# One block of gate and up by Strassen's scheme, SiLU as one ScalarE pass, and exchanges issued by GpSimd

## The chip, the core and the metric

The kernel runs on one core of a Trainium2 chip. The engines meant below are TensorE (PE, matmuls; its weight loads are listed as PEld), VectorE (DVE), ScalarE (ACT), GpSimd (POOL) and SyncE (SP, which here only issues DMAs). The metric is the device time of one execution in microseconds; three runs of the kernel before gave 575.81 us in the median (575.01 to 576.74).

## The reference, cut to what matters

One decoder layer on 256 tokens of width 1024, all in float32. The parts that the change touches are the feed-forward network (width 2816) and the gate at the end:

```python
x = x + (sigmoid(g_a) * y_a + sigmoid(g_b) * y_b) @ W_out
h2 = rms_norm(x, ln2_g[i])
g_ff, u_ff = jnp.split(h2 @ w_gate_up[i], 2, axis=-1)
x = x + (jax.nn.silu(g_ff) * u_ff) @ w_down[i]
h3 = rms_norm(x, ln3_g[i])
x = x + (p[i] @ w_ple_proj[i]) * jax.nn.sigmoid(h3 @ w_ple_gate[i])
```

`w_gate_up` is 1024 x 5632: 2816 columns of gate, then 2816 of up.

## The kernel before

**Matmuls in three terms.** Every float32 operand is split into a rounded high part (`wh`, `ah`) and the remainder (`wl`, `al`), and a product is the sum of three matmuls, `ah wh + ah wl + al wh` (`Panel.step`, issued by `mm` at L275). The tokens stand in two halves of 128, the columns in panels of 512, the inner dimension in pieces of 128. A panel holds one PSUM bank for each token half. Two pieces of weights, 128 x 2 x 512, make a tile: SP loads it (L395), ACT rounds it into `wh` (all ACT passes are recorded at L254), DVE subtracts to get `wl` (L377). Four buffers hold raw tiles, five `wh`, five `wl`. A tile serves 12 matmuls of 512 columns in an ordinary panel: two pieces, two token halves, three terms.

**Order.** The program text is written around PE. A filler (`Filler`) keeps a modelled time that each matmul advances, and runs side tasks (generators that yield the time at which they want to go on) between matmuls. The engines' queues are then laid out by priority: "w" (weight tiles) ahead of "ev" (work on finished panels) ahead of "bg" (background) ahead of the matmuls, each instruction as early as a model of the time finds it ready. Each engine executes its queue in order, so an instruction that waits holds all behind it.

**Gate and up** (L1497 to L1583). The feed-forward columns are cut into five blocks of 512 and one of 256. The first three panels (gate and up of block 0, gate of block 1) run interleaved; from then on `whole()` runs one panel as two halves of four pieces each. For the gate, `Gated.gate` takes a sigmoid on ACT with the row's `rstd2` as scale, and a DVE instruction multiplies the scaled panel with it (L1509). For up, one DVE instruction multiplies the panel in (L1518), DVE transposes within 32 x 32 blocks (L1527), and `send` moves the 32-row groups among the partitions with 16 DMAs from SP (L1537), so that the columns come to stand on partitions. After a lag of 26 us of modelled time `split` rounds the moved block (ACT) and takes the remainder (DVE, L1549), and the down projection can use it. Only after the last block's rows are split can the last chunk of the first down panel run.

**Norms.** `h2` is not divided by its row norm before the matmuls; the factor `rstd2` (one number per token, so two columns of 128) is applied to the finished panels. `rstd3` is used in the same way at the end.

**The end.** `pj` holds `p @ w_ple_proj`, copied from PSUM at L1489 long before. `final` (L1598) takes the sigmoid of the last panels on ACT, multiplies with `pj` (L1603), adds the residual (L1604) and stores.

Of the kernel before, what the change touches and what calls it, by code (L numbers as in the profile page):

```python
# [16 lines left out]
P = 128  # L17
# [46 lines left out]
NFF = 11  # L64

# [124 lines left out]
def tile_layer(ctx: ExitStack, tc: tile.TileContext, head, xk, pt, vec, w_dt, w_big, w_dn2, w_pp, out):  # L190
# [171 lines left out]
    def w_tiles():  # L362
        return (sb.tile([P, 2, 512], F32, tag="raw", bufs=RAW, name=nm("raw")),
                sb.tile([P, 2, 512], F32R, tag="wh", bufs=WH, name=nm("wh")),
                sb.tile([P, 2, 512], F32R, tag="wl", bufs=WL, name=nm("wl")))
# [1053 lines left out]
    class Residual:  # L1419
# [7 lines left out]
        def take(self, n, pan):  # L1427
# [51 lines left out]
    for n in range(2):  # L1479
        pan = Panel()  # L1480
        parts = load(w_pp[n], 2)
        for tt, pc in enumerate(pan.pieces):
            for k in range(2):
                pan.step(pc, parts[k], (p_h[:, k], p_l[:, k]), k == 1)
                if 4 * n + 2 * tt + k in SPLITS:
                    res2.split(*ready.pop(0))
        with prio("ev"):
            for tt in range(2):
                copy = nc.vector.tensor_copy(pj[n][:, tt], pan.ps[tt])  # L1489
                if n == 1:  # L1490

                    follow(copy.ins, fill.split)


    ff = []

    class Gated:  # L1497
# [4 lines left out]
        def gate(self, pan, c):  # L1502

            with prio("ev"):
                for tt, ps in enumerate(pan.ps):
                    r = rstd2[:, tt : tt + 1]
                    f = s2([self.w])
                    act(f, ps[:, c], AF.Sigmoid, scale=r)
                    stt(f, ps[:, c], r, f, op0=ALU.mult, op1=ALU.mult)  # L1509
                    self.f.append(f)  # L1510
# [20 lines left out]
        def send(self, turned):  # L1531
            n = self.both.shape[3]
            moved = s4([4, 2 * n])
            with prio("ev"):
                for a in range(4):
                    for b in range(4):
                        nc.sync.dma_start(  # L1537
                            moved[32 * b : 32 * b + 32, a], self.both[32 * a : 32 * a + 32, b].rearrange("p t n -> p (t n)"))
            fill.spawn(self.split(moved.rearrange("p a (x j) -> p x a j", j=32)), 0)

        def split(self, moved):

            yield fill.now + (26000.0 if self.w > 256 else 26500.0)
# [7 lines left out]

    behind = iter([(None, None), (fill.rounded, fill.rounded)])
    pans = [Panel(), Panel(aside=True), Panel()]
# [9 lines left out]

    def whole():
# [6 lines left out]
    gated = Gated(512)  # L1571
    gated.gate(pans[0], WHOLE)
    gated.up(pans[1], WHOLE)
    for n in range(1, NFF // 2):
# [3 lines left out]
    pan = Panel()  # L1578
    for k in (0, 4):
        pan.add(next_chunk(), h2[k : k + 4], last=k == 4)  # L1580
# [4 lines left out]
    res3 = Residual(xin, V_G3, rstd3, False)  # L1585
    for n in range(2):
# [11 lines left out]
    def final(n, pan):  # L1598
        with prio("ev"):
            for tt, c, ps in pan.pieces:  # L1600
                t = s2([512])[:, c]
                act(t, ps, AF.Sigmoid, scale=rstd3[:, tt : tt + 1])
                nc.vector.tensor_mul(t, t, pj[n][:, tt, c])  # L1603
# [6 lines left out]
def _layout(i):  # L1610
# [36 lines left out]
    blocks[:2] = [[np.concatenate(pairs[k : k + 2], axis=1) for k in range(0, 12, 2)], blocks[1][2:]]  # L1647
    rest = np.concatenate([w[:, 512 * (NFF // 2) :][:, :256] for w in (gu, ups)], axis=1)
# [41 lines left out]
```

## Time and profile before

| | |
|---|---|
| median of three runs | 575.81 us (575.01 to 576.74) |
| the profiled execution | 574.76 us, span 572.8 us |
| granted TensorE clock | 1.0 |
| PE busy | 567.3 us, 99% of the span |
| weight loads busy | 476.0 us, 83% |
| DVE busy | 444.5 us, 78% |
| ACT busy | 339.7 us, 59% |
| POOL busy | 88.0 us, 15% |
| DMA | 121.22 MB, mean 212 GB/s |

The trace gives each instruction with its line, its start from the span's beginning, its duration, and the idle time of its engine before it with what ended that idle time. A row such as `1.06 ACT ... [1.66 <-PE g L275]` says that ACT ran 1.06 us after 1.66 us without work, and that PE at line 275 released it. Matmul durations overlap, because they are pipelined; the distance between their starts is what one costs.

### The profile page before, as it was taken

The page shows a single profiled execution, that of the slowest core. Times are in us where ns is not written, and L with a number is a line of the kernel's source. Part 1 is how long each engine was busy: PE and PEld are TensorE (multiplying, and loading weights), DVE is VectorE, ACT ScalarE, POOL GpSimd, SP SyncE. Part 2 cuts the span into 40 slices and gives each one's busy share as a digit, 9 for nine tenths or more (in the row PEclk, how much of TensorE's full clock was granted, in tenths as well). Part 3 has the DMA queues.
Part 4 walks back from the last instruction along what each step waited for, and adds up shares of the span by engine and source line. Part 5 has one row for each costly group of instructions (what it writes and reads, how often), then busy time and mean ns, then how long its engine had stood idle before and what let it go on. Part 6 is the DMA issues. An engine that isn't in the chain of part 4 may idle for free.

```text
span 572.8 us, 8553 instructions
## 1 busy us (share of the span) xinstructions
PE 567.3 (99%) x2971; PEld 476.0 (83%) x2971; DVE 444.5 (78%) x702; ACT 339.7 (59%) x532; POOL 88.0 (15%) x127
## 2 busy tenths in 40 slices
PE   9999999999999999999999999999999999999996
PEld 8887898988888888888887888888888888888885
DVE  6678899989999988898695976766767767556565
ACT  6855567676779579748574454646355445444452
POOL 2011223000533403211320200300000000002020
PEclk9999999999999999999999999999999999999999
DMA  8875698656476756757655785575677666657652
GB/s 317 325 265 175 222 266 238 208 153 180 156 191 185 208 177 173 257 162 249 186 168 190 267 287 194 167 273 184 197 238 242 210 214 233 219 190 256 196 173 73
DMA packets 43802, 121.22 MB, mean 212 GB/s; under 512 B 6384, under 2 KB 14608, under 8 KB 43760
## 3 DMA queue, kind: packets, MB, share of 16 engines
q1 hardware_dynamic: 39040, 107.71, 57.0%
q0 software_dynamic: 4144, 12.32, 8.6%
q10 hardware_dynamic: 576, 0.66, 0.4%
q8 instruction: 23, 0.38, 0.3%
q14 instruction: 19, 0.16, 0.1%
HBM read 111.28 MB, written 6.44 MB: 205 GB/s over the span
## 4 chain that ended last, share of the span: by engine, by line
PE 98%; DMA 1%; DVE 0%; ACT 0%; issue 0%
PE g L275 88%; PE pb L275 8%; PE pb L297 2%; DMA raw<-in_head 1%; ACT s L254 0%; DVE s L1603 0%; DVE s L1604 0%; DVE wh L373 0%
## 5 line engine op out<-in xcount | busy, mean ns | idle before, releaser
L275 PE MATMUL g<-wh,s 128*128 128x512 f32 (+1 forms) x1220 | 381.8, 390 | 0.1
L254 ACT ACTIVATE wh<-raw 128x1024 fp32r<-128x1024 f32 (+2 forms) x192 | 198.9, 1039 | 159.5 <-PE g L275 125.0
L377 DVE TENSOR_TENSOR wl<-raw,wh 128x1024 fp32r<-128x1024 f32 (+2 forms) x188 | 223.6, 1194 | 81.4 <-ACT wh L254 73.3
L275 PEld LDWEIGHTS g<-wh,s 128*128 128x128 f32 x1220 | 228.7, 189 | 47.5 <-issue 0.5
L275 PE MATMUL g<-wl,s 128*128 128x512 f32 (+1 forms) x610 | 235.6, 388 | 0.0
L275 PEld LDWEIGHTS g<-wl,s 128*128 128x128 f32 x610 | 114.6, 188 | 23.2 <-issue 0.4
L275 PE MATMUL g<-s,wh 128*128 128x512 f32 (+1 forms) x320 | 90.3, 353 | 0.0
L275 PE MATMUL g<-s,wl 128*128 128x256 f32 x256 | 69.2, 283 | 0.0
L275 PEld LDWEIGHTS g<-s,wh 128*128 128x128 f32 x320 | 54.8, 190 | 6.8 <-DVE s L1392 0.3
L275 PEld LDWEIGHTS g<-s,wl 128*128 128x128 f32 x256 | 48.5, 189 | 2.0 <-issue 0.2
L254 ACT ACTIVATE s<-s 128x512 f32<-128x512 f32 (+4 forms) x45 | 34.9, 786 | 17.6 <-DVE s L1432 5.6
L749 POOL DMA_DIRECT2D turn_d<-s x16 | 12.6, 788 | 194.9 <-DVE s L739 194.5
L275 PEld LDWEIGHTS pb<-s,s 128*64 128x64 f32 (+2 forms) x336 | 23.9, 158 | 5.8 <-issue 2.4
L275 PE MATMUL pb<-s,s 128*64 128x128 f32 (+5 forms) x336 | 28.7, 294 | 0.0
L254 ACT ACTIVATE s<-pb 128x512 f32<-128x512 f32 (+3 forms) x45 | 20.3, 481 | 13.7 <-PE pb L275 8.4
L254 ACT ACTIVATE s<-s,vecs 128x256 f32<-128x256 f32 (+1 forms) x48 | 23.3, 536 | 6.3 <-DMA s<-turn_d 5.3
L653 DVE SCALAR_TENSOR_TENSOR s<-s,vecs,s 128x255 f32<-128x255 f32 (+2 forms) x60 | 26.4, 478 | 0.0
L759 POOL DMA_DIRECT2D s<-turn_d x40 | 22.5, 595 | 25.3 <-DMA turn_d<-s 10.3
L886 POOL TENSOR_SCALAR_AFFINE_SELECT rr<-a_h 128x512 fp32r<-128x512 f32 x16 | 16.8, 1134 | 37.9 <-PE pb L275 21.6
L254 ACT ACTIVATE s<-s,tiny 128x128 f32<-128x128 f32 (+1 forms) x44 | 18.7, 444 | 5.9 <-DVE tiny L1086 5.9
L254 ACT ACTIVATE s<-g 128x256 f32<-128x256 f32 (+1 forms) x44 | 20.0, 472 | 1.3 <-PE g L275 1.3
L794 POOL TENSOR_TENSOR tiny<-tiny,mhalf 128x8 f32<-128x8 f32 x8 | 13.2, 1649 | 42.0 <-DVE tiny L792 41.6
(153 smaller groups left out, 382.0 us busy)
## 6 DMA issues: line engine op xcount, KB each, us to landing
raw<-in_w_big SPq DMA_DIRECT2D x176, 512.0 KB
turn_d<-s POOLq DMA_DIRECT2D x14, 256.0 KB, 4.7
s<-turn_d POOLq DMA_DIRECT2D x28, 128.0 KB, 4.9
wl<-in_w_big POOLq DMA_DIRECT2D x5, 512.0 KB, 8.0
s<-s SPq DMA_DIRECT2D x80, 32.0 KB
raw<-in_head SPq DMA_DIRECT2D x4, 512.0 KB
s<-in_xk SPq DMA_DIRECT2D x4, 512.0 KB
raw<-in_head SPq DMA_DIRECT2D x6, 256.0 KB
```

The source lines that it names most:

```text
L254: return nc.scalar.activation(o, i, f, **kw)
L275: ins = nc.tensor.matmul(o, lhsT, rhs, start=start, stop=stop).ins
L297: queue(nc.tensor.transpose(o, i, ident[: i.shape[0], : i.shape[0]]).ins, main)
L377: low = nc.vector.tensor_sub(wl, raw, wh.bitcast(F32))
L653: stt(cc[j][:, sft:], pu[:, j, : T - sft], cw[j][3 - sft], cc[j][:, sft:], op0=ALU.mult, op1=ALU.add)
L749: nc.gpsimd.dma_start(d[:, :, at : at + t_.shape[2]].rearrange("b p n -> p b n"), t_)
L759: by[via[b % len(via)]].dma_start(o[32 * b : 32 * b + 32], d[b].rearrange("(a i) n -> i a n", i=32))
L794: nc.gpsimd.tensor_tensor(f, ms, mhalf, op=ALU.pow)
L886: nc.gpsimd.affine_select(r, bcast(a_h[:, c, h0 : h0 + 4].bitcast(F32), P), pattern=[[0, 4], [1, P]], compare_op=ALU.is_ge, fill=0.0, base ...
```

## The change

1. **One block of gate and up by Strassen's scheme (the variant with seven products and shared sums).** For the block of columns 1536 to 2047 the product is seen as a 2 x 2 product: the activations A in two token halves by two halves of the inner dimension, the weights B as gate and up by the same halves of the inner dimension. Instead of eight products of such blocks, seven are made, P1 to P7, each one PSUM bank and 12 matmuls of 512 columns. The sums of activations are made once in `wino_rows`: the second token half is scaled by the ratio of the two halves' norms, broadcast to all partitions by a small matmul, so that one factor `rstd2[:, 0:1]` serves all products; GpSimd adds high and low parts, DVE makes the sums and ACT and DVE split them. The sums of weights come by accumulating DMAs issued by GpSimd onto a held tile: P1 uses the first weight block, then the next is added, for P5, P6 and P4; a second chain serves P3 and P7; P2 uses a plain tile. `GatedWino.run` combines the products on DVE (one product on GpSimd).
2. **Its place.** The seven products are not run in a row: `whole()` runs one step ahead of each half panel from the third half on. The weights of this block now come first in the order of blocks.
3. **SiLU.** `Gated.gate` is one ACT pass with SiLU and no DVE instruction. The final sigmoid becomes 0.5 (tanh(z / 2) + 1): the scale is half of `rstd3`, `pj` is stored halved, and DVE's product becomes a fused (t + 1) x `pj`.
4. **The exchanges.** `send`'s 16 DMAs are issued by GpSimd, in four groups of four with 2 us of modelled time between, and the split's lag is shortened by the 8 us that the groups take.

```diff
+GAP = 2000.0
+WINO_FROM = 2
...
+                        if not self.normed:
+                            nc.gpsimd.tensor_scalar(hrstd3[:, tt : tt + 1], self.dst[:, tt : tt + 1], 0.5, None, op0=ALU.mult)
...
-                copy = nc.vector.tensor_copy(pj[n][:, tt], pan.ps[tt])
+                copy = nc.vector.tensor_scalar(pj[n][:, tt], pan.ps[tt], 0.5, None, op0=ALU.mult)
...
+    def wino_rows():
+        yield fill.now + 12000.0
+        while len(res2.acts[0]) < 4:
+            yield fill.now + 500
+        with prio("bg"):
+            ratio = tiny([1])
+            nc.vector.reciprocal(ratio, rstd2[:, 0:1])
+            nc.vector.tensor_mul(ratio, ratio, rstd2[:, 1:2])
+            rd = s2([P])
+            nc.vector.tensor_scalar(rd, ident, ratio, None, op0=ALU.mult)
+            pr = pb([P])
+            mm(pr, ones, rd, True, True)
+            prs = s2([P])
+            act(prs, pr)
+            a1, a2 = s4([2, 4, P]), s4([2, 4, P])
+            for h in range(2):
+                for k in range(4):
+                    hi, lo = (x.bitcast(F32) for x in res2.acts[h][k][:2])
+                    ptt(a2[:, h, k], hi[:, P:], lo[:, P:], op=ALU.add)
+                ptt(a2[:, h], a2[:, h], prs.unsqueeze(1).to_broadcast([P, 4, P]), op=ALU.mult)
+            for h in range(2):
+                for k in range(4):
+                    hi, lo = (x.bitcast(F32) for x in res2.acts[h][k][:2])
+                    ptt(a1[:, h, k], hi[:, :P], lo[:, :P], op=ALU.add)
+            for p, h in (("P1", 0), ("P2", 1)):
+                wino_ops[p] = [(hi[:, :P], lo[:, :P]) for hi, lo, _ in res2.acts[h]]
+        yield fill.now + 6000
+        with prio("bg"):
+            q, q_h, q_l = (sb.tile([P, 4, P], dt, tag="rr", bufs=4, name=nm("rr")) for dt in (F32, F32R, F32R))
+            nc.vector.tensor_sub(a1[:, 0], a2[:, 0], a1[:, 0])
+            nc.vector.tensor_sub(q, a1[:, 0], a2[:, 1])
+            nc.vector.tensor_add(a1[:, 1], a1[:, 1], q)
+            nc.vector.tensor_sub(a2[:, 0], a2[:, 0], a2[:, 1])
+            for a, ps in ((a1, ("P7", "P3")), (a2, ("P5", "P4")), (q, ("P6",))):
+                h, l = (s4([2, 4, P], F32R) for _ in range(2)) if a is not q else (q_h, q_l)
+                follow(act(h, a).ins, fill.cast)
+                nc.vector.tensor_sub(l, a, h.bitcast(F32))
...
+    class Wino:
+        TAKES = {"P1": ("q", "b11"), "P5": ("q", "b12"), "P6": ("q", "b22"), "P4": ("q", "b21"),
+                 "P3": ("r", "b22"), "P7": ("r", "b12"), "P2": (None, "b21")}
+        NEXT = {"P1": "P5", "P5": "P6", "P6": "P4", "P3": "P7"}
...
+        def load(self, p):
+            chain, b = self.TAKES[p]
+            parts = []
+            with prio("w"):
+                for i, src in enumerate(self.srcs[b]):
+                    if chain is None:
+                        tiles = w_tiles()
+                        nc.sync.dma_start(tiles[0], src)
+                    else:
+                        if (chain, i) not in self.held:
+                            self.held[chain, i] = s4([2, 512])
+                            nc.sync.dma_start(self.held[chain, i], src)
+                        tiles = (self.held[chain, i], *w_tiles(1))
+                    fill.cast = split_w(tiles).ins
+                    if p in self.NEXT:
+                        nc.gpsimd.dma_start(tiles[0], self.srcs[self.TAKES[self.NEXT[p]][1]][i], accum_op=ALU.add)
+                    parts += parts_of(tiles)
+            return parts
+
+        def product(self, p, ps=None, begin=True, end=True):
+            parts = self.load(p)
+            fill.drain(lambda: len(self.acts.get(p, ())) == len(parts))
+            if ps is None:
+                ps = pb([512])
+            for k, ((wh, wl), (ah, al)) in enumerate(zip(parts, self.acts[p])):
+                with prio("mm"):
+                    mm(ps, ah, wh, begin and k == 0, False, main=True)
+                    mm(ps, ah, wl, False, False, main=True)
+                    mm(ps, al, wh, False, end and k == len(parts) - 1, main=True)
+                fill.step()
+            return ps
...
-                    act(f, ps[:, c], AF.Sigmoid, scale=r)
-                    stt(f, ps[:, c], r, f, op0=ALU.mult, op1=ALU.mult)
+                    act(f, ps[:, c], AF.Silu, scale=r)
...
         def send(self, turned):
-            n = self.both.shape[3]
+            fill.spawn(self.moves(self.both), 0)
+
+        def moves(self, both):
+            n = both.shape[3]
             moved = s4([4, 2 * n])
-            with prio("ev"):
-                for a in range(4):
+            for a in range(4):
+                with prio("ev"):
                     for b in range(4):
-                        nc.sync.dma_start(
-                            moved[32 * b : 32 * b + 32, a], self.both[32 * a : 32 * a + 32, b].rearrange("p t n -> p (t n)"))
-            fill.spawn(self.split(moved.rearrange("p a (x j) -> p x a j", j=32)), 0)
+                        nc.gpsimd.dma_start(
+                            moved[32 * b : 32 * b + 32, a], both[32 * a : 32 * a + 32, b].rearrange("p t n -> p (t n)"))
+                yield fill.now + GAP
+            yield from self.split(moved.rearrange("p a (x j) -> p x a j", j=32))
...
-            yield fill.now + (26000.0 if self.w > 256 else 26500.0)
+            yield fill.now + (26000.0 if self.w > 256 else 26500.0) - 4 * GAP
...
+    class GatedWino(Gated):
+        def run(self):
+            product = self.wino.product
+            r = rstd2[:, 0:1]
+            p1 = product("P1")
+            with prio("ev"):
+                v1, c11, f1 = s2([512]), s2([512]), s2([512])
+                act(v1, p1, scale=r)
+            yield
+            p3 = product("P3")
+            yield
+            p5 = product("P5")
+            yield
+            p2 = product("P2")
+            with prio("ev"):
+                stt(c11, p2, r, v1, op0=ALU.mult, op1=ALU.add)
+                act(f1, c11, AF.Silu)
+            yield
+            p6 = product("P6")
+            with prio("ev"):
+                stt(v1, p6, r, v1, op0=ALU.mult, op1=ALU.add)
+                c12 = s2([512])
+                stt(c12, p5, r, v1, op0=ALU.mult, op1=ALU.subtract)
+                stt(c12, p3, r, c12, op0=ALU.mult, op1=ALU.add)
+                ptt(f1, f1, c12, op=ALU.mult)
+            yield
+            p7 = product("P7")
+            with prio("ev"):
+                stt(v1, p7, r, v1, op0=ALU.mult, op1=ALU.subtract)
+                c22 = s2([512])
+                stt(c22, p5, r, v1, op0=ALU.mult, op1=ALU.add)
+                turned = [self.turn(f1, 0)]
+            yield
+            p4 = product("P4")
+            with prio("ev"):
+                stt(v1, p4, r, v1, op0=ALU.mult, op1=ALU.subtract)
+                f2 = s2([512])
+                act(f2, v1, AF.Silu)
+                nc.vector.tensor_mul(f2, f2, c22)
+                self.send(turned + [self.turn(f2, 1)])
+            yield
...
         for k in (0, 4):
+            if half_no[0] >= WINO_FROM:
+                gw.step()
+            half_no[0] += 1
             pan.add(next_chunk(), h2[k : k + 4], last=k == 4)
...
-                act(t, ps, AF.Sigmoid, scale=rstd3[:, tt : tt + 1])
-                nc.vector.tensor_mul(t, t, pj[n][:, tt, c])
+                act(t, ps, AF.Tanh, scale=hrstd3[:, tt : tt + 1])
+                stt(t, t, 1.0, pj[n][:, tt, c], op0=ALU.add, op1=ALU.mult)
...
+    blocks = [blocks[0], blocks[3], *[b for i, b in enumerate(blocks) if i not in (0, 3)]]
```

The weight blocks reach the sums by addition alone, so P5 reads b11 + b12, P6 that plus b22, P4 that plus b21, P7 b22 + b12; the signs are in the activations' sums and in `run`. A further helper in the diff, `wino_acts`, is defined and not called.

More of the change, by code (lines that the diff above doesn't have):

```diff
@@ L360, in tile_layer, with w_tiles @@
     chunk_no = [0]
[L362 to L365, printed above, removed]
+    def w_tiles(first_=0):
+        return [sb.tile([P, 2, 512], dt, tag=tag, bufs=bufs, name=nm(tag))
+                for tag, dt, bufs in (("raw", F32, RAW), ("wh", F32R, WH), ("wl", F32R, WL))[first_:]]
     def split_w(tiles, js=slice(0, 2), c=WHOLE, on=None):
@@ L1495, in tile_layer @@
     ff = []
+    wino_ops = {}
+    def wino_rows():
[35 more added lines that the diff above has]
+                nc.vector.tensor_sub(l, a, h.bitcast(F32))
+                for i, p in enumerate(ps):
+                    hp, lp = (h, l) if a is q else (h[:, i], l[:, i])
+                    wino_ops[p] = [(hp[:, k], lp[:, k]) for k in range(4)]
@@ new lines, in blocks_of, with wino_acts, tiles, take @@
+    def blocks_of(t):
+        return t.rearrange("p n (a j) -> p n a j", a=4)
+    def wino_acts(a11, a12, a21, a22, ops, rank, own=("P1", "P2", "P4")):
+        n = a11.shape[1]
+        two = n == 2
+        def tiles(dt):
+            if two:
+                t = s4([4, n, P], dt)
+                return [t], [t[:, i] for i in range(4)]
+            ts = [s4([2, n, P], dt) for _ in range(2)]
+            return ts, [t[:, i] for t in ts for i in range(2)]
+        def take(p, hi, lo):
+            ops.setdefault(p, []).extend((hi[:, k], lo[:, k]) for k in range(n))
+        def plain(p, a, new):
+            o = new([2, n, P], F32R)
+            follow(act(blocks_of(o[:, 0]), a).ins, fill.cast)
+            nc.vector.tensor_sub(blocks_of(o[:, 1]), a, blocks_of(o[:, 0].bitcast(F32)))
+            take(p, o[:, 0], o[:, 1])
+        with prio(rank):
+            whole32, (q, s4_, s1, m3) = tiles(F32)
+            vtt = nc.vector.tensor_tensor
+            vtt(blocks_of(m3), a21, a11, op=ALU.subtract)
+            vtt(blocks_of(q), blocks_of(m3), a22, op=ALU.subtract)
+            vtt(blocks_of(s4_), a12, blocks_of(q), op=ALU.add)
+            vtt(blocks_of(s1), a21, a22, op=ALU.subtract)
+            for p, a in (("P1", a11), ("P2", a12), ("P4", a22)):
+                if p in own:
+                    plain(p, a, s2 if two else s4)
+            his, hi = tiles(F32R)
+            los, lo = tiles(F32R)
+            for w, h, l in zip(whole32, his, los):
+                follow(act(h, w).ins, fill.cast)
+                nc.vector.tensor_sub(l, w, h.bitcast(F32))
+            for i, p in enumerate(("P6", "P3", "P5", "P7")):
+                take(p, hi[i], lo[i])
@@ L1550, in split, with __init__, step @@
             ff.extend((fh[:, :, i], fl[:, :, i]) for i in range(n))
+    class GatedWino(Gated):
+        def __init__(self, srcs):
+            super().__init__(512)
+            self.wino = Wino(wino_ops, srcs)
+            self.steps = iter(self.run())
+        def step(self):
+            next(self.steps, None)
+        def run(self):
[38 more added lines that the diff above has]
+            yield
     behind = iter([(None, None), (fill.rounded, fill.rounded)])
+    fill.spawn(wino_rows(), 0)
     pans = [Panel(), Panel(aside=True), Panel()]
@@ L1562, in tile_layer, with wino_srcs @@
     h2 = res2.acts[0] + res2.acts[1]
+    def wino_srcs():
+        srcs = {}
+        for b in ("b11", "b21", "b12", "b22"):
+            src = next_src()
+            srcs[b] = [src[:, k : k + 2] for k in (0, 2)]
+        return GatedWino(srcs)
+    gated = Gated(512)
+    gated.gate(pans[0], WHOLE)
+    gated.up(pans[1], WHOLE)
+    half_no = [0]
     def whole():
@@ L1567, in whole @@
         for k in (0, 4):
+            if half_no[0] >= WINO_FROM:
+                gw.step()
+            half_no[0] += 1
             pan.add(next_chunk(), h2[k : k + 4], last=k == 4)
         return pan
[L1571 to L1574, printed above, removed]
+    gw = wino_srcs()
+    for n in range(1, NFF // 2 - 1):
         gated = Gated(512)
@@ L1577, in tile_layer @@
         gated.up(whole(), WHOLE)
-    pan = Panel()
-    for k in (0, 4):
-        pan.add(next_chunk(), h2[k : k + 4], last=k == 4)
+    pan = whole()
     gated = Gated(256)
@@ L1585, in tile_layer @@
     res3 = Residual(xin, V_G3, rstd3, False)
+    hrstd3 = const.tile([P, 2], F32, name="hrstd3")
     for n in range(2):
```

2 lines of the change are left out of this document (added).

## The prediction

> **What bounds the kernel now.** I read the page's busy times and chain first, then the chain in order of time over the gate and up stage, then busy times by stretch, then the queues of ScalarE (ACT), VectorE (DVE), SyncE (SP) and GpSimd (POOL) in that stage.
>
> ```profile
> PE 567.3 (99%) x2971; PEld 476.0 (83%) x2971; DVE 444.5 (78%) x702; ACT 339.7 (59%) x532; POOL 88.0 (15%) x127
> PE 98%; DMA 1%; DVE 0%; ACT 0%; issue 0%
> ...
> 38.22 0.43 PE pb L275 x2
> ...
> 388.38 5.44 PE g L275 x24
> ...
> 396.54 157.11 PE g L275 x696
> ```
>
> TensorE (PE) is the chain, from 4.3 us to 568.3 us; other engines end nothing but the last 2 us. The 24 matmuls of one half panel take 5.44 us, 0.2267 us each. The change lives from 363.9 (the three interleaved panels) over 396.5 (whole panels) to 483.6 us (down projection begins).
>
> ```profile
> 100.00:200.00 100.00, 100.00 (x646) 86.11 (x645) 94.77 (x188) 71.00 (x137) 24.72 (x24) 1.00 0.61 183
> ...
> 363.90:396.50 32.60, 32.60 (x148) 27.00 (x147) 21.05 (x28) 19.06 (x24) 3.22 (x7) 1.00 0.63 214
> 396.50:407.40 10.90, 10.90 (x50) 9.03 (x49) 9.33 (x12) 5.52 (x6) 0.00 (x0) 1.00 0.51 164
> 407.40:464.50 57.10, 57.10 (x254) 47.28 (x253) 39.54 (x41) 28.36 (x29) 0.00 (x0) 1.00 0.69 222
> ```
>
> The columns are length, then busy time of PE, weight load, DVE, ACT, POOL (instructions in brackets), granted clock, DMA share, GB/s. PE has no idle time and the clock is 1.00, so a removed matmul is 0.2267 us off the span as long as its successors' operands are there. DVE has room (39.5 of 57.1 us), POOL does nothing there.
>
> How far are operands ahead?
>
> ```profile
> 448.25 1.06 ACT L254 ACTIVATE wh<-raw 128x1024 fp32r<-128x1024 f32 x1 [1.66 <-PE g L275]
> 449.35 1.23 DVE L377 TENSOR_TENSOR wl<-raw,wh 128x1024 fp32r<-128x1024 f32 x1 [1.50 <-ACT wh L254]
> ```
>
> ACT's cast waits for PE: it refills one of five `wh` buffers the moment PE frees it, and the low half is done 450.58 - 448.25 = 2.3 us later. Four tiles of 12 matmuls (2.72 us) stand before it: a lead of 10.9 - 2.3 = 8.6 us. A stall of DVE or ACT shorter than that costs PE nothing.
>
> **Part 1: eight block products become seven.** The block's 96 matmuls (two panels, two token halves, eight k pieces, three terms) become seven products of 12, so 84. Removed: 12 x 0.2267 = 2.72 us on the path. Added to PE: the broadcast of the rstd ratio (`mm(pr, ones, rd)`), 128 moving columns; the same matmul with 256 takes 0.43 us in the chain above, so between 0.11 (a quarter) and 0.43; I take half, 0.22.
>
> **Part 2: what the seven products need.** Fourteen weight tiles are cast and subtracted for this block in place of eight; held tiles become the next combination by an accumulating DMA that POOL issues (eight of them).
>
> ```profile
> L1509 DVE SCALAR_TENSOR_TENSOR s<-g,rstd,s 128x512 f32<-128x512 f32 x10 | 7.5, 745 | 4.5 <-ACT s L254 4.5
> L1527 DVE STREAM_TRANSPOSE s<-s 128x512 f32<-128x512 f32 x10 | 7.1, 706 | 0.1
> ...
> s<-turn_d POOLq DMA_DIRECT2D x28, 128.0 KB, 4.9
> wl<-in_w_big POOLq DMA_DIRECT2D x5, 512.0 KB, 8.0
> ...
> L399 POOL DMA_DIRECT2D wl<-in_w_big x5: 922/947/971, 88.7 to 221.4; - x5
> ```
>
> A step of the block (2 tiles, 2.72 us) alternates with an ordinary half panel (2 tiles, 5.44 us): seven times 8.16 = 57.1 us, 28 tiles where 21 ran. DVE in it: 28 subtractions x 1.23 = 34.4; seven fused multiply-adds on the products and four for two ordinary blocks' ups, 11 x 0.745 = 8.2; one product 0.7; six transposes x 0.706 = 4.2; two splits of returned rows x 1.23 = 2.5: 50.0 us, 88%. The stretch from 100 to 200 us shows 94.8% with PE never idle, so I book 0; the lead there is four tiles of 2.04 us less 2.3 = 5.9 us. ACT: 28.4 us now, seven more casts x 1.06 and two passes of at most 0.7 over products: 37 of 57.1. The sums of activations add about 6 us of DVE before 407 us, where 30.4 of 43.5 us are busy. DMA: 222 GB/s x 57.1 us = 12.7 MB, plus 7 x 0.52 MB, gives 16.4 MB, 286 GB/s; the first two slices of the page, where PE is the chain too, ran 317 and 325 GB/s.
>
> ```profile
> GB/s 317 325 265 175 222 266 238 208 153 180 156 191 185 208 177 173 257 162 249 186 168 190 267 287 194 167 273 184 197 238 242 210 214 233 219 190 256 196 173 73
> ```
>
> The longest chain, P1, P5, P6, P4 on one pair of held tiles: cast 1.06, subtraction 1.23, issue 0.95, landing 8.0 = 11.2 us, against 16.3 us of PE between their uses. No cost booked; above 16.3 + 5.9 it reaches PE.
>
> **Part 3: SiLU and tanh on ACT.** Two DVE instructions per gate (10 of 0.745, two of 0.48) go: 8.4 us of DVE off the path. ACT's instruction stays one pass.
>
> ```profile
> L254 ACT ACT_TABLE_LOAD x2 | 2.6, 1283 | 2.1 <-PEq L1679 1.7 <-PE g L275 0.3
> ...
> 568.79 0.42 DVE L1603 TENSOR_TENSOR s<-s,s 128x256 f32<-128x256 f32 x1 [0.45 <-ACT s L254]
> ...
> L1509 DVE SCALAR_TENSOR_TENSOR s<-g,rstd,s 128x256 f32<-128x256 f32 x2 | 1.0, 480 | 0.9 <-ACT s L254 0.9
> ```
>
> In the tail the fused (t + 1) x pj replaces a product, 0.48 for 0.42: +0.06 on the path. No row shows which functions share a table: between no further load and one ahead of the first tanh, 1.28 us on ACT with four more pieces of panel to come before the end. Either way 0 there. The halvings of pj and of rstd3 ride on a pass that exists and on an idle POOL.
>
> **Part 4: exchanges from SP to POOL.** 96 issues (16 a block, six blocks) leave SP's queue; PE never waited for what stood behind them there, so nothing is gained. On POOL the nearest rows are the reads back from DRAM and the writes to it:
>
> ```profile
> L759 POOL DMA_DIRECT2D s<-turn_d x40: 551/556/912, 73.4 to 529.8; - x40
> ...
> L749 POOL DMA_DIRECT2D turn_d<-s x16: 750/763/980, 66.2 to 521.7; - x16
> ...
> 489.61 0.45 DVE L1527 STREAM_TRANSPOSE s<-s 128x256 f32<-128x256 f32 x1
> ...
> 507.31 0.63 ACT L254 ACTIVATE s<-s 128x512 fp32r<-128x512 f32 x1 [0.88 <-DMA s<-s]
> ```
>
> Only the last exchange is tight: transposed at 490.06, its rows were awaited until 507.31, and the split ends near 508.7, when the last down chunk needs it. On POOL, 16 x 0.556 to 0.79 = 8.9 to 12.6 us, and up to 1.3 us behind the block before it, then up to 4.9 us to land (the exchange through DRAM above): 503.9 to 508.9. So between nothing and 1.6 us late. I take 0, by L759, whose destinations also have 32 partitions. The groups of four let the accumulating issues between.
>
> **Sum.** -2.72 + 0.22 + 0.06 = -2.44 us. Against the profiled execution, 574.76 us (span 572.8 and 2.0 around it): 572.3. That execution lies 1.05 below the median; the median of the runs, 575.81, gives **573.4**.
>
> **Rivals.** About 0.3% (1.7 us) is what a measurement can tell here; the forecast keeps "faster" if less than 0.7 us of stalls comes back.
>
> *A, GpSimd's sums hold up DVE (slower).* Eighteen POOL operations (16 adds of 128 columns, two products of 512) feed DVE's subtractions, which stand in DVE's queue 6 us of PE work later with all weight splits behind them.
>
> ```profile
> L886 POOL TENSOR_SCALAR_AFFINE_SELECT rr<-a_h x16: 624/974/3708, 89.4 to 224.1; 128x512 fp32r<-128x512 f32 x16
> ...
> L886 POOL TENSOR_SCALAR_AFFINE_SELECT rr<-a_h 128x512 fp32r<-128x512 f32 x16 | 16.8, 1134 | 37.9 <-PE pb L275 21.6 <-DVE wl L377 16.3
> ...
> L377 DVE TENSOR_TENSOR wl<-raw,wh x38: 1180/1226/1226, 398.6 to 498.3; 128x1024 fp32r<-128x1024 f32 x38
> ```
>
> One POOL form takes from 0.62 to 3.71 us beside a busy DVE, while L377's durations stay 1.18 to 1.23. No row shows an add of two operands of this size. Eighteen at 0.62 are 11.2 us, and DVE would stand 5.2, inside the lead: nothing. Eighteen at L886's mean of 1.13 are 20.4 us: DVE would stand 20.4 - 6 = 14.4 us, PE 14.4 - 8.6 = 5.8 us, result 579.2. Above 6 + 8.6 + 2.44 = 17.0 us of POOL time it is slower than before. Against it: DVE is 65% busy there, not 95%. The Trainium skill (SBUF — State Buffer, Who interferes with whom) says that a DVE instruction with two SBUF inputs and a GpSimd one that reads SBUF lock each other out for a whole instruction; L886's spread agrees, and every L377 has two SBUF inputs. By the busy share alone the sums take 11 us and the time stays 573.4; by the rule at its worst, each of the eighteen waiting out one 1.23 us subtraction, they take 33 us, and the estimate is 592. Chance of A 0.17.
>
> *B, the steps take tiles faster than they come.* One step lasts 2.72 us, two tiles cost DVE 2.46, and an accumulated tile may land late at 286 GB/s. For it: the lead shrinks to 5.9 us, and DVE's multiply-adds wait in order for products that PE has just ended, with the weight splits queued behind them. Against: DVE's 94.8% elsewhere. If each of the seven steps loses 0.25 us, 1.75 comes back: 575.1, no change. Chance 0.17.
>
> *C, the last exchange is late on POOL.* Its upper bound, 1.6 us, goes one for one into PE: 575.0. Chance 0.07.
>
> *D, the change does not do what it says:* more table loads than one, as between SiLU and each cast, 28 x 1.28 = 36 us of ACT on top of 37 in 57.1: 16 us late, 589. Nothing speaks for it: sigmoid alternated with casts under two loads. Chance 0.02.
>
> **How the numbers follow.** Forecast 0.57, at 573.4, own range 572.5 to 574.0. Faster: the forecast, 0.57, and a little of B, 0.01. Same: most of B, C, 0.21. Slower: A, D and the rest of B, 0.21. The low end is 575.81 - 2.72, less the median's distance to the lowest run, 0.8: 572.2. The high end takes in B, C and half of A: 577.8.
>
> **What would show it.** Right: PE without idle time, gate and up ending near 481.1 us, POOL some 70 us busier, L1509 gone, two table loads. Wrong by A: DVE idle for a POOL line at 385 to 405 us, then PE waiting for `wl`. By B: PE waits inside the steps, between 407 and 464 us. By C: PE waits near 505 us. Any PE wait over 0.7 us ends the forecast.

## The result, and the profile after

The changed kernel takes 583.33 us in the median (582.30 to 584.41), the kernel before 575.41 us on the same chip: a ratio of 1.0136 (95% interval 1.0108 to 1.0165), 7.9 us slower. The forecast was 573.4 us, 2.4 faster. Medians here and below are of all executions, ratios of the fast ones alone: a few executions ran in a slower state, among them two of the twelve in experiment 9, without which its median is 573.14 us, and one in experiment 12. The profiled execution has a span of 580.6 us against 572.8.

The page of the kernel after, busy times and the chain's shares by engine:

```profile
PE 568.8 (98%) x2961; PEld 474.5 (82%) x2961; DVE 455.2 (78%) x712; ACT 347.1 (60%) x543; POOL 161.7 (28%) x252
PE 72%; DMA 14%; DVE 5%; issue 4%; POOL 3%; ACT 1%; SPq 0%; ACTq 0%; POOLq 0%; DVEq 0%
```

The chain that was 98% PE now has DMA, DVE, issue and POOL in it. Where, the chain in order of time shows (start, duration, what):

```profile
377.93 2.95 PE pb L277 x14
380.88 5.48 PE g L277 x24
...
394.53 2.72 PE pb L277 x12
...
403.31 0.59 POOL s L1674
...
420.02 0.40 POOL s L1614
...
421.17 11.94 DMA s<-in_w_big
433.19 1.07 ACT wh L256
...
435.43 1.23 DVE wl L378
436.67 8.30 DMA raw<-in_w_big
445.08 1.07 ACT wh L256
...
447.45 5.51 PE g L277 x23
...
472.00 81.75 PE g L277 x360
```

The broadcast of the rstd ratio is the row of 14 matmuls: 2.95 us in place of 2.72. From 402.7 us the chain goes through GpSimd's queue: moves of gated rows (L1674), an accumulating transfer (L1614, 11.94 us to land), ACT's cast of the tile it fills, and behind that cast the ordinary raw tiles. TensorE's own timeline has these waits, all the waits between 397 and 472 us (the bracket is idle time and its end):

```profile
413.60 0.50 PE L277 MATMUL pb<-wl,s 128*128 128x512 f32 x1 [2.53 <-DVE wl L378]
...
430.66 0.50 PE L277 MATMUL pb<-wh,s 128*128 128x512 f32 x1 [0.67 <-ACT wh L256]
431.92 0.50 PE L277 MATMUL pb<-wl,s 128*128 128x512 f32 x1 [0.76 <-DVE wl L378]
...
434.30 0.49 PE L277 MATMUL pb<-wh,s 128*128 128x512 f32 x1 [0.94 <-ACT wh L256]
435.56 0.50 PE L277 MATMUL pb<-wl,s 128*128 128x512 f32 x1 [0.77 <-DVE wl L378]
...
447.45 0.50 PE L277 MATMUL g<-wl,s 128*128 128x512 f32 x1 [0.43 <-DVE wl L378]
```

The first is in P1, the next four in P5, the last in the half panel after P2: 6.10 us together. The stretches that answer to those of the prediction, in the same columns:

```profile
407.40:464.50 57.10, 51.01 (x212) 40.30 (x211) 38.37 (x39) 30.65 (x33) 23.80 (x42) 0.97 0.90 243
435.00:440.00 5.00, 4.44 (x12) 3.53 (x13) 5.00 (x6) 3.98 (x5) 0.86 (x1) 0.66 1.07 223
```

The 57.1 us had 254 matmuls and now have 212. Behind the waits the granted clock is 0.66 and 12 matmuls fill 4.44 us: 12 x (0.37 - 0.2267) = 1.7 us more. A matmul ahead of a wait takes 0.39 us, and the one behind it 0.34 to the next start, where a stream has 0.2267 from start to start: 0.28 for each of the six waits. So the waits of 6.10 us cost 6.1 + 1.7 + 1.7 = 9.5 us. The run with plain tiles (below) says the same: its stretch from the row at 393.36 us to the row at 461.36 us is 68.0 us where this one's is 472.00 - 394.53 = 77.5. With -2.72 for the matmuls, +0.27 for the broadcast (2.95 and 5.48 in the chain), 0.4 us by which this execution was behind that of the kernel before ahead of the block (369.77 against 369.33 us in the two chains; no cause was found, and the profiled executions of all the runs differ by up to 1.9 us there), and a wait of 0.29 us near the end, that makes the 7.8 us between the spans.

The Trainium skill (TensorE: Matmul & The Clock Gate, What's actually happening) says that the clock is halved after about 3.4 us without work and comes back after as long a time of work. The first experiment agrees, with a clock of 0.50 behind a wait of 6.37 us. This kernel does not: its slow stretch stands behind four waits of 0.67 to 0.94 us, none of them near 3.4.

**Why the operands were late.** GpSimd's timeline:

```profile
403.31 3.05 POOL L1674 DMA_DIRECT2D s<-s  x6 [16.15 <-PE g L277]
...
411.16 3.07 POOL L1674 DMA_DIRECT2D s<-s  x6 [1.10 <-DMA s<-s]
...
417.57 2.46 POOL L1674 DMA_DIRECT2D s<-s  x5 [0.73 <-issue]
420.02 0.97 POOL L1614 DMA_DIRECT2D s<-in_w_big  x1
...
421.17 1.28 POOL L1614 DMA_DIRECT2D s<-in_w_big  x1
```

and SyncE's, ScalarE's and VectorE's, one after the other:

```profile
402.51 3.06 SPq L1610 DMA_DIRECT2D s<-in_w_big  x4
```

```profile
409.14 1.06 ACT L256 ACTIVATE wh<-s 128x1024 fp32r<-128x1024 f32 x1 [8.44 <-DMA s<-in_w_big]
411.05 1.06 ACT L256 ACTIVATE wh<-s 128x1024 fp32r<-128x1024 f32 x1 [0.85 <-DMA s<-in_w_big]
...
429.55 1.06 ACT L256 ACTIVATE wh<-s 128x1024 fp32r<-128x1024 f32 x1 [1.55 <-DMA s<-in_w_big]
...
433.19 1.06 ACT L256 ACTIVATE wh<-s 128x1024 fp32r<-128x1024 f32 x1 [2.02 <-DMA s<-in_w_big]
...
445.08 1.06 ACT L256 ACTIVATE wh<-raw 128x1024 fp32r<-128x1024 f32 x1 [6.10 <-DMA raw<-in_w_big]
```

```profile
412.36 2.32 DVE L378 TENSOR_TENSOR wl<-s,wh 128x1024 fp32r<-128x1024 f32 x2
...
430.64 1.23 DVE L378 TENSOR_TENSOR wl<-s,wh 128x1024 fp32r<-128x1024 f32 x1 [9.14 <-ACT wh L256]
```

Three things are to be seen. The first held tiles are loaded only at 402.5 us, and P1's first matmul, which needs only the high part, ran at 410.68. Its tiles are split at 413.6 and 414.7, so that their sums could start, but 25 of the 32 moves of blocks 0 and 1 stand ahead on GpSimd's queue (and one more between the two transfers), which are issued at 420.0 and 421.2. And ACT, which works in order, stands before a gate panel until 427.3 us and then twice before a held tile (1.55 and 2.02 us) while the raw tiles behind them wait; raw buffers are not freed, SyncE loads no further tile, and at 445 us a raw tile is missing too.

### The profile page after: what moved, and what is told of

The parts are those of the page before. It is cut to its first block, busy times and chain, and to the rows that moved or that the text cites. A ratio compares the mean times of both kernels' runs of the same rounds, so it can differ in the third digit from the quotient of the medians.

```text
span 580.6 us, 8614 instructions
## 1 busy us (share of the span) xinstructions
PE 568.8 (98%) x2961; PEld 474.5 (82%) x2961; DVE 455.2 (78%) x712; ACT 347.1 (60%) x543; POOL 161.7 (28%) x252
## 4 chain that ended last, share of the span: by engine, by line
PE 72%; DMA 14%; DVE 5%; issue 4%; POOL 3%; ACT 1%; SPq 0%; ACTq 0%; POOLq 0%; DVEq 0%
PE g L277 62%; PE pb L277 9%; DMA raw<-in_w_big 4%; DVE wl L378 2%; DMA s<-in_w_big 2%; PE pb L299 2%; DMA s<-s 2%; DMA wl<-in_w_big 2%; DMA raw<-in_head 2%; POOL tiny L795 2%; DMA turn_d<-s 2%; ACT wh L256 1%; DMA s<-turn_d 1%; POOL s L1674 1%; DVE s L1360 1%
## 5 line engine op out<-in xcount | busy, mean ns | idle before, releaser
L277 PE MATMUL g<-wh,s 128*128 128x512 f32 (+1 forms) x1156 | 364.2, 391 | 0.4 <-ACT s L256 0.3
L256 ACT ACTIVATE wh<-raw 128x1024 fp32r<-128x1024 f32 (+2 forms) x186 | 191.8, 1038 | 136.0 <-PE g L277 97.1
L378 DVE TENSOR_TENSOR wl<-raw,wh 128x1024 fp32r<-128x1024 f32 (+2 forms) x182 | 218.4, 1208 | 61.0 <-ACT wh L256 59.9
L277 PEld LDWEIGHTS g<-wh,s 128*128 128x128 f32 x1156 | 217.2, 189 | 45.9 <-ACT s L256 0.9
L277 PE MATMUL g<-wl,s 128*128 128x512 f32 (+1 forms) x578 | 223.7, 389 | 0.4 <-DVE wl L378 0.4
L277 PEld LDWEIGHTS g<-wl,s 128*128 128x128 f32 x578 | 108.7, 188 | 22.9 <-DVE wl L378 0.9
L1674 POOL DMA_DIRECT2D s<-s x96 | 48.6, 512 | 48.9 <-PE g L277 16.2
L256 ACT ACTIVATE s<-s 128x512 f32<-128x512 f32 (+4 forms) x49 | 38.2, 789 | 19.8 <-DVE s L1433 5.2
L277 PE MATMUL pb<-wh,s 128*128 128x512 f32 (+1 forms) x96 | 30.5, 378 | 1.6 <-ACT wh L256 1.6
L795 POOL TENSOR_TENSOR tiny<-tiny,mhalf 128x8 f32<-128x8 f32 x8 | 15.9, 1985 | 41.9 <-DVE tiny L793 41.9
```

The source lines that it names most:

```text
L256: return nc.scalar.activation(o, i, f, **kw)
L277: ins = nc.tensor.matmul(o, lhsT, rhs, start=start, stop=stop).ins
L378: low = nc.vector.tensor_sub(wl, raw, wh.bitcast(F32))
L795: nc.gpsimd.tensor_tensor(f, ms, mhalf, op=ALU.pow)
L1674: nc.gpsimd.dma_start(moved[32 * b : 32 * b + 32, a], both[32 * a : 32 * a + 32, b].rearrange("p t n -> p (t n)"))
```

## The experiments

Two theories were set against each other first: Q, the queue (moves ahead of the accumulating transfers), and D, the DMA engines (the transfers are slow by themselves while the engines are full). All times are medians; each ratio is to the kernel before on the same chip.

**1. The moves by SyncE again.**

```diff
-                        nc.gpsimd.dma_start(
+                        nc.sync.dma_start(
```

> Only the 96 moves of gated rows go back from GpSimd's queue to SyncE's; the Strassen block, its accumulating transfers and SiLU stay. Theory Q (the queue): GpSimd's queue holds 32 moves of blocks 0 and 1 from 403 to 426 us, so the accumulating transfers of the product P5, whose tiles were split at 412.4 and 414.7 us, are issued only at 420.0 and 421.2 and land at 429.5 and 433.1; with the moves gone they are issued within about 1 us of the split, P5 to P4 lose nothing, and of the 9.5 us that TensorE loses between 407 and 469 us only the 2.53 us wait ahead of P1 stay: about 583.3 - 7 = 576.3 us. Theory D (the DMA engines are full, share 1.05 between 425 and 445 us): the same bytes move, the accumulating transfers still land some 10 us after issue, and at most 2 us come back: 581 us or more.

Measured: 593.27 us, ratio 1.0323 (1.0298 to 1.0348). Neither theory had that. Its SyncE timeline, its waits of TensorE, its stretch behind the first wait, and its DMA queues from 400 to 470 us (packets, MB, share of the 16 engines):

```profile
401.13 9.21 SPq L1674 DMA_DIRECT2D s<-s  x12
410.44 1.00 SPq L1610 DMA_DIRECT2D s<-in_w_big  x2
```

```profile
415.81 0.79 PE L277 MATMUL pb<-wh,s 128*128 128x512 f32 x1 [6.37 <-ACT wh L256]
...
528.88 0.79 PE L277 MATMUL g<-wh,s 128*128 128x512 f32 x1 [8.93 <-ACT s L256]
```

```profile
415.00:420.00 5.00, 3.72 (x8) 2.63 (x9) 3.69 (x4) 3.81 (x5) 1.21 (x2) 0.50 0.88 252
```

```profile
q1 hardware_dynamic: 4649, 11.38, 49.3%
q0 software_dynamic: 1152, 4.19, 32.1%
```

The moves now stand ahead of the loads of the held tiles: P1 waits 6.37 us instead of 2.53, and the clock is 0.50 after it. The last block's rows are 8.93 us late in the down projection. P5, though, does not wait at all, which is what Q says of it; P2, whose tiles are plain, waits 0.54, 0.76 and 0.61 us at 444 to 448 us. And q0 carries nothing here but the eight accumulating transfers: 32.1% for 4.19 MB is 7.66% per MB, where plain loads and moves on q1 take 49.3 / 11.38 = 4.33: an accumulating transfer keeps the DMA engines busy 1.77 times as long for the same bytes.

**2. No Strassen block.** The block is one more ordinary `Gated(512)`; SiLU, tanh and the moves by GpSimd stay.

```diff
-    fill.spawn(wino_rows(), 0)
...
-            if half_no[0] >= WINO_FROM:
-                gw.step()
```

> The Strassen block is undone (its activation sums, its products and the order of the weight blocks too); SiLU, tanh and the moves issued by GpSimd in groups of four stay. Theories Q and D both have the loss in the seven products: 575.4 us within 0.5, TensorE without idle time from 396 to 484 us, and GpSimd's queue late for nobody. Rival S (the moves by GpSimd or the new activation functions cost by themselves, by late gated rows or by table loads): 577 us or more, with TensorE waiting for split rows or for ScalarE.

Measured: 574.62 us, ratio 0.9998 (0.9984 to 1.0012). The whole loss is the block's. SiLU, tanh and the moves cost nothing by themselves; GpSimd's queue there, with nobody waiting for it, shows how moves are issued:

```profile
435.81 3.91 POOL L1674 DMA_DIRECT2D s<-s  x8 [12.61 <-issue]
440.14 1.48 POOL L1674 DMA_DIRECT2D s<-s  x3 [0.41 <-DMA s<-s]
```

Eight go out at 0.49 us each; after that the queue waits for earlier ones to land.

**3. The block with plain tiles.**

```diff
-        TAKES = {"P1": ("q", "b11"), "P5": ("q", "b12"), ...
-        NEXT = {"P1": "P5", "P5": "P6", "P6": "P4", "P3": "P7"}
+        TAKES = {"P1": (None, "b11"), "P5": (None, "b12"), ...
+        NEXT = {}
```

> Left out: the sums of weight blocks. Each of the seven products loads its two tiles plainly by SyncE into the ordinary raw buffers, so that the count of matmuls, casts and subtractions is that of the changed kernel but no accumulating transfer and no held tile exists. Theory Q and theory D: the chain of held tiles alone makes the loss, so TensorE idles under 0.7 us and the time is 575.4 - 2.4 = 573.0 us. Rival R (fourteen tiles in 57 us are more than the loads, ScalarE and VectorE bring up): waits of about 0.25 us or more in most steps, 575 to 580 us.

This kernel leaves out the weight sums and so does not compute the layer. Measured: 571.82 us, ratio 0.9946 (0.9929 to 0.9963), 2.85 us faster. Its stretch and its DMA queues (400 to 470 us):

```profile
407.40:464.50 57.10, 57.10 (x254) 47.28 (x253) 43.97 (x44) 33.67 (x35) 20.40 (x40) 1.00 0.80 261
```

```profile
q1 hardware_dynamic: 4565, 16.62, 72.9%
q0 software_dynamic: 1536, 1.58, 6.8%
```

Seven products with fourteen tiles run without a wait: rival R falls, and the loss is in the weight sums. More bytes per second than in the changed kernel (261 against 243 GB/s) at a lower share (0.80 against 0.90). GpSimd's 1.58 MB of moves take 4.3% per MB, as plain loads do (4.4), so it is the addition that costs, not that GpSimd issues it.

**4. The sums by VectorE.**

```diff
+                            raw, *rest = w_tiles()
+                            nc.sync.dma_start(raw, src)
+                            nc.vector.tensor_add(self.held[chain, i], self.held[chain, i], raw)
...
-                    if p in self.NEXT:
-                        nc.gpsimd.dma_start(tiles[0], ..., accum_op=ALU.add)
```

> The eight weight sums are made by VectorE from a plainly loaded raw tile, in place of eight accumulating transfers; the moves stay on GpSimd. VectorE's load in the 57.1 us of the steps rises from 51.0 by eight additions of about 1.2 us to 60.8. Theory Q: the waits of P5 to P4 for GpSimd's transfers go, the 2.53 us ahead of P1 stay, and VectorE's excess of 3.7 us is inside the 5.9 us of lead or costs up to 3.7: 576 to 580 us. Theory D: the same, since an ordinary load reads and writes less than an accumulating one. Rival R: VectorE is the bound from the first step on, and 583 us or more result.

Measured: 582.62 us, ratio 1.0141 (1.0103 to 1.0179), above what Q and D both gave. P1 waits 2.52 us as before, and P5 to P4 do not wait; the split of a half panel's tile is 1.75 us late at 462 us, where VectorE has no idle time; and in the down projection TensorE waits 2.09 and 0.71 us at 514 us for the splits of moved rows (experiment 6 shows why). All eight sums on VectorE gain nothing. That its load is the reason is not shown: it is busy for 48.2 of the 57.1 us, and the additions also take raw buffers, of which there are four.

**5. Held tiles of P1 earlier.** In the loop over the interleaved panels, at their third step:

```diff
+            first_held.extend(s4([2, 512]) for _ in range(2))
+            with prio("w"):
+                for i, t in enumerate(first_held):
+                    nc.sync.dma_start(t, w_big[chunk_no[0] + 1][:, 2 * i : 2 * i + 2])
```

> Only the two held tiles of P1 are loaded earlier: their loads stand in SyncE's queue between the tiles of the interleaved panels, some 14 loads sooner. The wait of 2.53 us ahead of P1 goes. Theory Q (the moves of gated rows stand in GpSimd's queue ahead of the accumulating transfers, which are issued at 420.0 and 421.2 us whatever the tile's split was): P5 comes due 2.5 us earlier and waits that much longer, so the time stays at 583.3 us, within 1. Theory H (the loss begins with the late held tiles and the rest follows from it): P5's transfers move forward with the split and 7 to 9 us come back, 574 to 576 us.

Measured: 588.87 us, ratio 1.0244 (1.0222 to 1.0266). P1 waits no more, but P3 does: its own held tiles are now loaded at 412.11 us, behind two raw loads more (at 407.65 and 411.73 us).

```profile
422.77 0.80 PE L277 MATMUL pb<-wh,s 128*128 128x512 f32 x1 [3.91 <-ACT wh L256]
```

P6 waits 1.75 us more, and the down projection 2.09 and 0.72. Both expectations were wrong. The transfers for P5 did move forward, to 410.5 and 413.8 us, behind 14 and 16 moves, since the queue was laid out anew, and P5 did not wait; so Q was wrong that they would stay, and H that the rest would come back with them. Early tiles for one product move the shortage to the next held tile.

**6. The sums first on GpSimd's queue.**

```diff
+            if sends[0] - 1 in (1,):
+                while len(accums) < 8:
+                    yield fill.now + 500
...
+                        follow(sent.ins, accums[-1].ins if accums else None)
```

> Only the order on GpSimd's queue is changed: the 16 moves of block 1 stand behind the eight accumulating transfers; block 0's 16 stay ahead of them. All bytes and instructions are the same. Theory Q: the transfers for P5 are issued at about 414.5 us in place of 420.0 and 421.2, land 10 us later, ahead of P5's turn; the waits in P5 and the slow clock behind them go, the 2.53 us ahead of P1 stay: about 576.3 us. Theory D (transfers that add to memory take too long by themselves while the DMA engines are full): P5 still waits, 580 us or more.

Measured: 583.57 us, ratio 1.0154 (1.0130 to 1.0178). The steps of it:

```profile
414.28 0.94 POOL L1615 DMA_DIRECT2D s<-in_w_big  x1 [0.17 <-PE pb L277]
415.69 0.88 POOL L1615 DMA_DIRECT2D s<-in_w_big  x1 [0.48 <-issue]
```

```profile
421.61 1.06 ACT L256 ACTIVATE wh<-s 128x1024 fp32r<-128x1024 f32 x1 [2.25 <-DMA s<-in_w_big]
425.56 1.06 ACT L256 ACTIVATE wh<-s 128x1024 fp32r<-128x1024 f32 x1 [2.89 <-DMA s<-in_w_big]
...
438.32 1.06 ACT L256 ACTIVATE wh<-raw 128x1024 fp32r<-128x1024 f32 x1 [4.23 <-DMA raw<-in_w_big]
```

```profile
513.40 0.50 PE L277 MATMUL g<-wh,s 128*128 128x512 f32 x1 [2.09 <-ACT s L256]
```

```profile
511.35 1.06 ACT L256 ACTIVATE wh<-raw 128x1024 fp32r<-128x1024 f32 x1 [1.66 <-PE g L277]
512.31 1.56 ACT L256 ACTIVATE s<-s 128x1024 fp32r<-128x1024 f32 x2
```

The transfers for P5 go out at 414.3 and 415.7, their tiles are cast 7.3 and 9.9 us later, and P5 waits for nothing: Q is right about P5. The total does not move, because the time was lost again in two places: raw tiles come late while ACT stood before the held ones (0.46, 0.54 and 0.77 us of TensorE at 440 to 444 us), and TensorE waits 0.37, 2.09 and 0.72 us in the down projection (3.2 us). There the moves as such are not late: those of the last block but one had all been issued by 495 us and landed some 4 us later. But ACT's queue has the split of these rows at 512.31 us, behind a weight cast that could start only when TensorE freed a buffer at 511.3, so that TensorE stands for the cast and the split, 1.06 and 1.04 us. Experiment 8 has this split two casts earlier, and no wait. What put it so late in the laid-out queue is open: the kernels of experiments 4 and 5, which hold no moves back, have the same order and the same 2.09 us.

**7. Both.** The edits of 5 and 6 together.

> Both: the held tiles of P1 loaded earlier and the moves of block 1 behind the eight accumulating transfers. Theory Q: no wait over 0.7 us is left in the steps, and the time is that of the plain tiles run or a little more: 572 to 574.5 us, below the kernel before. Theory D: P5 or P6 still wait for the transfers, 577 us or more. Theory H: no better than the early load alone.

Measured: 579.20 us, ratio 1.0075 (1.0056 to 1.0093). 0.28 and 0.59 us of wait are left in the steps, and 0.37, 2.09 and 0.72 us in the down projection.

**8. The moves of block 1 in the gap.** As 7, with `while len(accums) < 6`: the moves may go out while GpSimd waits for P6's tiles.

> As the run with the early load and the moves of block 1 behind the accumulating transfers, but behind six of the eight: the 16 moves go out in the stretch from 426 to 442 us, where GpSimd's queue waits 16.25 us for P6's tiles. Theory Q, in its second half (the moves held back are what made the down projection wait 0.37, 2.09 and 0.72 us between 502 and 511 us, through the chain of later moves on GpSimd's queue): these waits go, only the 0.9 us at 438 to 441 us stay, and 579.2 - 4 = 575 us results, within 1. Rival: the moves now stand ahead of P6's transfers (two of eight), which land late for P4, with a wait of 2 us or more at about 456 us: 577 us or more.

Measured: 574.33 us, ratio 0.9981 (0.9966 to 0.9996). The down projection waits no more, as Q had it; what the trace shows for it is the order on ACT's queue and no late move: the split of the last block but one runs at 503.26 us, where in experiment 7 it ran at 508.89, behind two more casts. 0.76, 0.53 and 0.75 us stay at 438 to 441 us. The row of the chain there:

```profile
426.77 11.77 DMA raw<-in_w_big
```

A plain load takes 11.8 us to land, while the share of the DMA engines is 1.05 to 1.06 between 425 and 435 us. This is what D would have left; experiments 10 and 12 do not confirm it. The Trainium skill (DMA: Bandwidth & Descriptors, Issuing engines are not separate DMA queues) says that DMAs of all issuing engines interleave on the same 16 engines and that another issuer saves only the time of the issue; these rows agree in kind: a load on SyncE's queue lands late while GpSimd's accumulating transfers are under way, and in experiment 4, which has none, loads in the chain landed in 4.7 to 6.9 us.

**9. A fifth raw tile**, and **10. two of the eight sums by VectorE.** As 8, each with one edit (in 10 the moves of block 1 stand behind four of six transfers, which is the same place):

```diff
-S2, S4, RAW, WH, WL = 13, 26, 4, 5, 5
+S2, S4, RAW, WH, WL = 13, 25, 5, 5, 5
```

```diff
+                        if p == "P7":
+                            nc.sync.dma_start(raw, src)
+                            nc.vector.tensor_add(tiles[0], tiles[0], raw)
...
-                    if p in self.NEXT:
+                    if p in self.NEXT and p != "P3":
```

> As the run with the moves in the gap, with five raw tiles in place of four and 25 of the general tiles in place of 26. Theory B5 (what is left in the steps comes from raw tiles: while ScalarE waits for a held tile no raw tile is freed, and SyncE loads none for 6 to 14 us): the wait of 0.9 us at 438 to 441 us goes, and the time is 1 us below that of the other, 573 to 574.5 us. Rival D (the DMA engines at a share of 1.03 to 1.06 between 410 and 435 us bring the tiles late whatever is free): the same time as the other.

> As the run with the moves in the gap, but the two sums from P3 to P7 are made by VectorE from plainly loaded raw tiles; six accumulating transfers stay. VectorE gets two additions of about 1.2 us in a stretch where it is busy for 42 to 44 of 57 us. Theory D (the accumulating transfers cost the DMA engines 1.8 times what a plain load costs for the same bytes, and their full share brings raw tiles late): the share falls below 1.0 between 415 and 435 us, the wait at 438 to 441 us goes, 573 to 574 us. Rival: VectorE's additions stand ahead of splits for products and cost as much as they save: 575 us or more.

Measured: 573.37 us, ratio 0.9968 (0.9958 to 0.9978), with the fifth tile; waits of 0.23 and 0.76 us are left. 575.15 us, ratio 0.9995 (0.9981 to 1.0009), with the two sums, as the rival had it and not D; 0.77 us in the steps and 0.37 us in the down projection. D was hardly put to the test: the DMA share from 415 to 435 us fell only from 1.04 to 1.01.

**11. The kernel before with the fifth raw tile**, and **12. edits 9 and 10 together.**

> The kernel before with five raw tiles in place of four and 25 general tiles in place of 26, nothing else. If the fifth raw tile helps only where held tiles stand in the way of raw ones, the kernel before, whose TensorE never waits, stays at 575.2 us within 0.5. If it is worth something by itself, 574 us or less, and the gain of the changed kernel with it is not the change's.

> The run with the fifth raw tile, and the two sums from P3 to P7 by VectorE from plain loads, so that six accumulating transfers stay. Theory D (what is left, 0.23 and 0.76 us at 440 us, comes from the DMA engines' full share of 1.03 to 1.06 between 430 and 445 us): the raw tiles come in time, no wait is left, 572.0 to 572.8 us. Rival: as between the runs with four raw tiles, the additions cost what the transfers did, 573 to 574 us.

Measured: 575.65 us, ratio 1.0010 (1.0000 to 1.0020), so the fifth tile is worth nothing without held tiles. And 574.09 us, ratio 0.9981 (0.9966 to 0.9995), though only 0.18 us of wait is left in the steps and the DMA share from 430 to 445 us is 0.95, against 1.04 in experiment 9: D's waits all but went, and the time did not follow, as the rival had it. The intervals of 9 and 12 overlap, so whether the two sums cost anything is open. The profiled execution of 12 reaches the interleaved panels 1.1 us later than that of experiment 3 (371.38 and 370.26 us at the same matmul), ahead of the whole block; runs with four raw tiles start this matmul anywhere from 370.00 to 371.55 us, so this need not come from the fifth tile.

The fastest kernel that computes the layer is number 9, 0.3% below the kernel before.

## Why the prediction was wrong

**Part 1 was right.** Without weight sums the time falls by 2.85 us (2.1 to 4.1 by the interval; 2.44 forecast), and the broadcast costs 0.27 (0.22).

**Part 2 failed, at "The longest chain, P1, P5, P6, P4 on one pair of held tiles: cast 1.06, subtraction 1.23, issue 0.95, landing 8.0 = 11.2 us".** The sum has no term for the queue. Counted as there, from one cast of a held tile to the next, the chain took 429.55 - 409.14 = 20.4 us for one tile of P1 and 433.19 - 411.05 = 22.1 for the other. The missing term is 6.4 and 6.5 us on GpSimd's queue behind the moves (413.6 to 420.0, 414.7 to 421.2). The other terms were too small: cast and subtraction took 4.5 and 3.6 us for 2.3, since VectorE had work on a panel ahead of the subtraction, and issue and landing 9.5 and 12.0 for 9.0 (the eight transfers landed in 7.3 to 13.5 us, 9.9 in the median). Experiment 6 took the queue term away: the chain was 14.4 and 16.6 us, and P5's waits went.

**The lead was a second failure of Part 2.** Both chains are just inside the 16.3 + 5.9 = 22.2 us that was to be the limit. P5 still waited, because the 5.9 us were not there. They were read from ordinary tiles, which are loaded four ahead and cast as soon as one of five `wh` buffers is free. A held tile has no such lead: its load stands wherever the queue has it, at 402.5 us for P1, whose split was 2.5 us late. And ACT's order makes the lead common: a held tile that is late takes the lead of all raw tiles behind it, so the wait is paid again at 447 us (or at 440 us in experiments 6 to 10).

**The DMA term of Part 2 was mis-sized.** 286 GB/s was compared with 317 and 325 on the page. Bytes were the wrong measure: an accumulating transfer costs 1.77 times the engine time of a plain one. 4.19 MB of them count like 7.4, and the share went to between 1.03 and 1.07 at 219 to 313 GB/s (425 to 445 us, in stretches of 5). VectorE's 50.0 us was on the high side: experiment 3, with all fourteen splits, has 43.97 in the same 57.1 us. Two small sums of the range do not come out either: its low end is 572.3, and its high end of 577.8 holds C and half of A, but not B; the result lies above it with B too.

**Part 4 was wrong where it says "The groups of four let the accumulating issues between".** In the queue as laid out, 25 moves go first; the layout follows a model of the time in which the tiles are split later than they were, or the moves are shorter than they are (which of the two was not tried). The moves as such cost nothing, as Part 4 said (experiment 2), and, with the block, SyncE's queue would not have been the better place (experiment 1).

**Part 3 was right**: no time in experiment 2, and two table loads in the trace, as many as before.

**The rivals.** *A* did not decide. GpSimd's eighteen sums took 14.7 us, under the point of 17.0; the groups, in the stretch from 366 to 390 us:

```profile
L1521 POOL TENSOR_TENSOR s<-s 128x128 f32<-128x128 f32 x8 | 6.5, 824 | 4.2 <-DVE s L1238 4.2
L1526 POOL TENSOR_TENSOR s<-s 128x128 f32<-128x128 f32 x8 | 5.7, 737 | 0.0
L1522 POOL TENSOR_TENSOR s<-s,s 128x512 f32<-128x512 f32 x2 | 2.5, 1293 | 0.1
```

One add takes between 0.45 and 1.45 us: those of 1.44 run from 377 to 384.5 us, while VectorE subtracts, and one that starts in VectorE's pause at 382.7 us takes 0.46. So VectorE does stretch them, but it waited only 1.7 us for them and TensorE not at all. *B* named the place and, with "an accumulated tile may land late", the mechanism; its price of 0.25 us a step, 1.75 in all, was chosen, not worked out from a queue, and the loss was 9.5. *C* did not show: TensorE waited for the last exchange only with the moves on SyncE's queue (8.93 us in experiment 1). The 2.09 us of experiments 4 to 7 are the split of an earlier block, late in ACT's queue. The sign that was to end the forecast, a wait of TensorE over 0.7 us, was there four times.

## What to carry to other kernels

When work is added to a queue, write out what will stand ahead of it there, with issue times and landings, and start the chain's sum at that point; the busy share of an engine (28% here) says nothing of it. Tiles with a path of their own need their own lead, and while they share an in-order engine with ordinary tiles, a late one takes the lead of all. When a wait is removed, look for the next one before counting the gain: here three positions on two queues had to be right together (579.2 and 583.6 us with less) before the 2.4 us that the matmuls are worth began to show.

## What the runs showed of the hardware

- A transfer that adds to its destination occupies the DMA engines for 7.66% per MB in a window of 70 us where plain transfers take 4.3 to 4.4, issued by SyncE or by GpSimd.
- After TensorE waited 6.37 us the granted clock was 0.50 in the 5 us that followed; after four waits of 0.67 to 0.94 us within 5 us it was 0.66. There the slow matmuls cost 1.7 us behind 3.1 us of waits. A single wait of 2.53 us left it at 1.00 in the changed kernel; in experiment 4, after one of 2.52 us, it was 0.80 from 410 to 415 us.
- In experiment 2 GpSimd's queue issued eight of these DMAs at 0.49 us each and then waited for earlier ones to land, so that 16 moves took 9 us (435.8 to 444.9); 29 moves with four accumulating transfers took 23 us in the changed kernel (403.3 to 426.6). Whether eight is a limit of the chip or of this program was not tried.
